# Premaking started later, operand steps and departures regrouped in the down products of an encoder block

## The chip, the cores and the metric

The kernel runs on one core of one Trainium2 chip. The metric is the device time of one execution in microseconds. Engines are named as in the profile: PE (TensorE), DVE (VectorE), ACT (ScalarE), POOL (GpSimd) and SP (SyncE, which only issues DMAs here).

## The reference

One encoder block for 2048 tokens of 1024 channels in float32, cut to what matters here:

```
h  = rmsnorm(x, norm1_g);  p = h @ w_in           # q, k, v, gate, two low-rank decays, u and v of the gMLP
yA = gla_mixer(...)          # chunked gated linear attention, forward and backward over the tokens
yB = gmlp_mixer(...)         # u * (W_s layernorm(v) + b), 128 positions mixed in each of 4 groups
x  = x + concat(yA, yB) @ w_out
h2 = rmsnorm(x, norm2_g)
x  = x + (silu(h2 @ w_gate) * (h2 @ w_up)) @ w_down     # d_ff = 2816
return rmsnorm(x, final_norm_g)
```

## The kernel before

**Tiles and precision.** The channels lie on the 128 partitions, so a block of TB = 512 tokens is KT = 8 tiles of 128x512. The tokens are NB = 4 such blocks. Each float32 product is made of three passes in a faster format, fp32r: every operand is split into a high part (a cast, mostly by ACT) and a low part (the rest, by DVE), and PE multiplies high by high, high by low and low by high.

**Phases.** The first one projects q, k and v and runs the attention forward. The third phase (C; some 310 to 690 us) goes through the blocks 3, 2, 1, 0. For each it makes the z products of the gMLP in a loop of four (the attention's backward steps, `backward`, run beside it: each loads o, ds and q for 128 tokens on SP, scales qb on POOL (L803) and multiplies it on PE as pob (L808)), then the gate and u products, then the eight out products `pout`, n = 0 to 7, with the residual added by DVE as xc (L924). Beside these the next block is normalised (c2h and c2l) and the squares of the new rows are summed (e3sq on ACT, e3a on DVE). The gate and up phase (some 690 to 1630 us) makes the products of a pair of blocks, (3, 2) and then (1, 0), by the Strassen-Winograd scheme: seven products in place of eight, in `seven`, named by slots 0 to 6. The last phase (some 1630 to 2075 us) makes the down products in the same way.

**The down products.** Each pair has three parts, c = 0, 1, 2, of 4, 4 and 3 k-tiles per half. A part is 28 products: one for each of seven slots and each of four column groups q. With 4 k-tiles a product is 12 matmuls of 128x512, with 3 it is 9. In parts 0 and 1 the order is slot 0 four times, slot 4 four times, then slots 3, 1, 2, 6, 5 for each q; in part 2 it is 0 and 4, then 1, 2, 5 for each q, then slot 3 four times and slot 6 four times. A product is named d_ with q and a letter of its bank (d_0e: q = 0). DVE adds the products into acc, one tile for each q, with the steps at L991 and L1152.

**What is loaded and made for them.** The right-hand operands of a part come from DRAM as ac (L1092, SP, eight pieces of 512 KB) and are turned into the seven slots by `moving`, in 22 *operand steps*, each a cast by ACT (L235) and a subtraction by DVE (L236), or one subtraction by DVE (L246). The low and high tiles are named by slot or place: tah and tal, tbh and tbl (slots 0 and 4), s2h and s2l, s5h and s5l, s6h and xf. The tuple `steps` says how many operand steps follow each product of a part; `loads` says after which products a piece of the next part is loaded; `fresh` says after which products the next part's slots 0 and 4 are made.

The left-hand operands of the down products, with the sums of the scheme and both their parts, are *premade* by `make_down` during the third and the gate and up phases: for each set two loads of 512 KB on POOL into mk (L316), seven casts on ACT (L339), four sums (L335) and seven subtractions (L322) on DVE, and the results go to DRAM as dw (L325, POOL). It is a generator: `drain(makes, 1)` runs it to the next `yield`. There are twelve sets (three parts by four q). Later SP loads the results as dn376h, dn376l and so on (L399), in the order of the products.

**The final norm and what leaves.** For one block t of a pair, `square` makes sq (ACT, L1200) of each finished row of acc, and DVE adds most of them into tot. `rstd` multiplies them with ones into fm (L1168, PE), takes the root (ACT, L1170) and the reciprocal (DVE, L1171), and spreads it on a diagonal as tot (L1172); `rows` turns that into rows, fr (L1178, PE), copied back to tot by ACT (L1180). `leave` multiplies acc by it (DVE, L1186) and sends the tile out (L1187). At the change of pairs acc is reused: `residual` (L1160, POOL) loads the next pair's x into it after the old tile has left.

**Order.** In the last phase every engine keeps the order in which the program is written (a chain of dependencies made behind `begin`); `at(n, ...)` puts a call behind product n of a part. PE's banks come from a pool of seven.

## Time and profile before

| | us |
|---|---|
| median of 3 runs | 2097.71 (2095.57 to 2097.91) |
| the profiled execution, its own time | 2099.51 |
| its span, first to last record | 2097.80 |
| PE busy | 2044.1 (97%) |
| DVE busy | 1463.7 (70%) |
| ACT busy | 906.4 (43%) |
| POOL busy | 291.1 (14%) |

The mean granted clock of PE over the span is 0.988. Busy shares are averages over phases with different limits; the list of waits and the table of stretches below show the places.

### The profile page before, as it was taken

What the parts mean: (1) busy time and instruction counts of PE and PEld (TensorE: products, weight loads), DVE (VectorE), ACT (ScalarE), POOL (GpSimd) and SP (SyncE); (2) the same over time, 40 slices, a digit from 0 to 9 for tenths busy, and PEclk for the clock granted to TensorE, in tenths of its full rate; (3) what the DMA queues carried; (4) which work ended last, traced back from release to release, by engine and by line L of the source; (5) the groups of instructions that cost most, each with busy time, mean ns of one, the idle gap of its engine ahead of it and who ended that gap; (6) DMA issues with size and microseconds to landing.
All of it is one profiled execution on the core that took longest, in us unless ns stands there. A gap on an engine that the chain in (4) does not pass through costs nothing. (4 is left out here: it accounts for less than half of the span.)

```text
span 2097.8 us, 25871 instructions
## 1 busy us (share of the span) xinstructions
PE 2044.1 (97%) x9432; PEld 1670.0 (80%) x9432; DVE 1463.7 (70%) x2272; ACT 906.4 (43%) x1560; POOL 291.1 (14%) x487
## 2 busy tenths in 40 slices
PE   8999999999999999999999999999999999899997
PEld 6787877778887888888888888888888888677876
DVE  6977666767767768687766976676667575676576
ACT  6765454464645644343333533333333221431233
POOL 0212223212121100021221001211110100020000
PEclk9999999999999999999999999999999999999998
DMA  8633335555575533254454243433442966687654
GB/s 297 202 113 133 97 136 176 196 190 201 198 268 197 183 121 106 84 177 149 153 176 166 76 146 111 146 138 120 148 147 94 343 220 226 231 312 259 246 173 164
DMA packets 123361, 367.96 MB, mean 175 GB/s; under 512 B 15712, under 2 KB 36064, under 8 KB 121056
## 3 DMA queue, kind: packets, MB, share of 16 engines
q1 hardware_dynamic: 91456, 253.02, 35.1%
q0 software_dynamic: 31632, 112.75, 14.8%
q8 instruction: 74, 1.21, 0.2%
q14 instruction: 55, 0.45, 0.1%
q10 hardware_dynamic: 144, 0.52, 0.1%
HBM read 271.34 MB, written 94.90 MB: 175 GB/s over the span
## 5 line engine op out<-in xcount | busy, mean ns | idle before, releaser
L1079 POOL DMA_DIRECT2D da<-q x88 | 47.6, 541 | 533.6 <-DVE q L1077 511.8
L1055 ACT ACTIVATE cg<-cg 128x512 f32<-128x512 f32 x66 | 41.7, 632 | 118.0 <-DVE cg L1053 117.6
L339 ACT CAST mk<-mk 128x512 fp32r<-128x512 f32 (+1 forms) x84 | 48.9, 583 | 69.0 <-DVE mk L335 50.9
L322 DVE TENSOR_TENSOR mk<-mk 128x512 fp32r<-128x512 f32 (+1 forms) x84 | 56.9, 677 | 15.9 <-DMA dw38l<-mk 2.5
L995 ACT COPY u2d<-d_0a 128x512 f32<-128x512 f32 x6 | 3.5, 584 | 145.7 <-PE d_0a L987 145.7
L235 ACT CAST tah<-ac 128x1024 fp32r<-128x1024 f32 (+1 forms) x24 | 23.4, 977 | 69.1 <-DMA ac<-da 67.5
L617 POOL TENSOR_SCALAR qs<-QK,misc 128x128 f32<-128x128 f32 x30 | 25.6, 856 | 150.8 <-DVE QK L568 76.7
L1077 DVE TENSOR_TENSOR q<-q,cg 128x512 f32<-128x512 f32 x66 | 45.2, 684 | 0.4
L924 DVE TENSOR_TENSOR xc<-pout,xc 128x512 f32<-128x512 f32 x32 | 21.9, 688 | 33.4 <-PE pout L113 33.2
L1200 ACT ACTIVATE sq<-acc 128x512 f32<-128x512 f32 x28 | 17.7, 631 | 61.9 <-DVE acc L1152 61.9
L236 DVE TENSOR_TENSOR tbl<-ac,tbh 128x1024 fp32r<-128x1024 f32 (+1 forms) x24 | 26.3, 1132 | 20.6 <-ACT tbh L235 20.6
L641 DVE SCALAR_TENSOR_TENSOR sf<-sf,misc,dsb 64x128 f32<-64x128 f32 x56 | 19.9, 355 | 23.3 <-ACT dsb L631 22.7
L1187 POOL DMA_DIRECT2D out_dram<-acc x8 | 5.8, 722 | 207.8 <-DVE acc L1186 205.9
L335 DVE TENSOR_TENSOR mk<-mk 128x512 f32<-128x512 f32 (+1 forms) x48 | 34.1, 709 | 0.2
L1152 DVE TENSOR_TENSOR acc<-vvd,acc 128x512 f32<-128x512 f32 x48 | 33.0, 688 | 0.8
L236 DVE TENSOR_TENSOR tal<-ac,tah 128x1024 fp32r<-128x1024 f32 (+1 forms) x24 | 27.0, 1129 | 4.0 <-ACT tah L235 4.0
L818 DVE SCALAR_TENSOR_TENSOR sb<-sb,misc,dsr 128x128 f32<-128x128 f32 x30 | 10.0, 345 | 25.5 <-PE pob L808 24.7
L803 POOL TENSOR_SCALAR qb<-qb,misc 128x128 f32<-128x128 f32 x30 | 19.0, 641 | 62.0 <-DMA qb<-dq 62.0
L624 ACT COPY ot<-po 128x256 f32<-128x256 f32 x32 | 10.3, 373 | 38.7 <-PE po L621 22.0
L246 DVE TENSOR_TENSOR ac<-ac,ac 128x1024 f32<-128x1024 f32 (+1 forms) x24 | 26.7, 1129 | 0.0
L246 DVE TENSOR_TENSOR ac<-ac 128x1024 f32<-128x1024 f32 (+1 forms) x24 | 26.5, 1128 | 0.0
L235 ACT CAST tbh<-ac 128x1024 fp32r<-128x1024 f32 (+1 forms) x24 | 22.5, 981 | 7.0 <-DVE ac L246 6.3
(4609 smaller groups left out, 7358.3 us busy)
## 6 DMA issues: line engine op xcount, KB each, us to landing
da<-q POOLq DMA_DIRECT2D x88, 256.0 KB, 2.3
ac<-da SPq DMA_DIRECT2D x40, 512.0 KB, 6.5
wo<-in_wo_dram SPq DMA_DIRECT2D x32, 512.0 KB, 4.3
xk<-in_xtok_dram SPq DMA_DIRECT2D x16, 512.0 KB, 6.1
wv<-in_wv_dram SPq DMA_DIRECT2D x16, 512.0 KB, 3.5
xc<-in_xT_dram SPq DMA_DIRECT2D x4, 2048.0 KB, 9.6
wg<-in_wg_dram SPq DMA_DIRECT2D x16, 512.0 KB, 3.5
wz<-in_wz_dram SPq DMA_DIRECT2D x16, 512.0 KB, 3.6
```

Source lines behind the costliest of these rows:

```text
L235: nc.scalar.copy(out=hi[:, c, :], in_=src[:, c, :])
L236: nc.vector.tensor_tensor(out=lo[:, c, :], in0=src[:, c, :], in1=hi[:, c, :].bitcast(F32), op=ALU.subtract)
L246: nc.vector.tensor_tensor(out=o[:, c, :], in0=a[:, c, :], in1=b[:, c, :], op=ALU.subtract)
L322: here(nc.vector.tensor_tensor(out=lo.bitcast(F32R), in0=src, in1=hi, op=ALU.subtract))
L335: here(nc.vector.tensor_tensor(out=how[0], in0=how[1], in1=how[2], op=how[3]))
L339: here(nc.scalar.copy(out=hi.bitcast(F32R), in_=src))
L617: nc.gpsimd.tensor_scalar_mul(qs[:, m, :], qd[m][:, c], ech[:, m, 2 * g:2 * g + 1])
L924: nc.vector.tensor_tensor(out=xt[:, n, :], in0=p, in1=xt[:, n, :], op=ALU.add)
L1055: nc.scalar.activation(out=o, in_=a, func=AF.Silu)
L1077: nc.vector.tensor_tensor(out=q, in0=a, in1=cg[:, 2 * m + t, :], op=ALU.mult)
L1079: nc.gpsimd.dma_start(out=d_a[pair[t]][j // KT][:, j % KT, :], in_=q)
L1152: nc.vector.tensor_tensor(out=o, in0=a, in1=o, op=ALU.add)
```

## The change

What it does, in seven pieces:

- *Premaking.* The third phase makes three sets instead of four, and lets four drain steps pass between the loads of a set and its first cast instead of two. Nothing is drained in block 3's z loop, so the first load is issued in its u loop. The gate and up phase makes four sets beside its first pair (as before, but the sets 3 to 6) and five beside its second (50 steps instead of 40).
- *Sums of the norm.* `rstd` first multiplies all terms but the last for four columns, then the last term for four others; ACT copies the first four and DVE adds the second. For pair 0's first block it stands one product later.
- *Pair change.* The first block of pair 0 leaves behind products 25, 26, 27, 27 of its last part (24 to 27 before); the second leaves behind products 4, 5, 13, 15 of the next part (3 to 6 before). Acc is reloaded by one DMA of 512 KB for both halves (`both`) instead of two. The early adds of the first slot in pair 1 stand behind product 13 + q (8 + q before). The operand steps of that part are regrouped.
- *Last parts.* In part 2 the operand steps are 3, 3, 3, 3, 2 instead of seven times 2.
- *Last part of pair 0.* The next part's pieces are loaded behind products 9 to 21 (7 to 20 before) and its slots 0 and 4 made behind 13, 14, 17, 19 (12, 13, 15, 17 before).
- *Last pair.* Two of the four tiles of its first block leave behind products 25 and 26, two behind the last product.
- *Output.* The result is written as (block, partition, tile, token), 4 KB in one piece for each partition of an output DMA, and brought into the reference's form outside the kernel.

```diff
--- before.py
+++ after.py
@@ -50,11 +50,10 @@
     wgu: bass.AP,
     wds: bass.AP,
     wdt: bass.AP,
-    outT: bass.AP,
+    outB: bass.AP,
 ):
     nc = tc.nc
     xv = xT.rearrange("(k p) t -> p k t", p=P)
-    ov = outT.rearrange("(k p) t -> p k t", p=P)
 
     cst = ctx.enter_context(tc.tile_pool(name="cst", bufs=1))
     xp = ctx.enter_context(tc.tile_pool(name="xp", bufs=1))
@@ -305,7 +304,7 @@
 
     d_w = [[drp.tile([P, D], F32, tag=f"dw{j}{x}", name=f"dw{j}{x}") for x in "hl"] for j in range(len(DOWN) // 2)]
 
-    def make_down(c, q, room):
+    def make_down(c, q, room, gap):
 
         hk = PARTS[c]
         w = hk * P
@@ -315,8 +314,8 @@
         for x, r in ((ra, 0), (rb, 1)):
             here(nc.gpsimd.dma_start(out=x, in_=wds[c, 2 * q + r] if c < 2 else wdt[2 * q + r]))
         c1, c2 = slice(0, w), slice(w, 2 * w)
-        yield
-        yield
+        for _ in range(gap):
+            yield
 
         def low(o, src, hi):
             here(nc.vector.tensor_tensor(out=lo.bitcast(F32R), in0=src, in1=hi, op=ALU.subtract))
@@ -344,9 +343,9 @@
 
     MADE = [(c, q) for c in range(len(PARTS)) for q in range(KT // 2)]
 
-    def make_downs(sets, room):
+    def make_downs(sets, room, gap=2):
         for x in sets:
-            yield from make_down(*x, room)
+            yield from make_down(*x, room, gap)
 
     class Stationary:
 
@@ -769,7 +768,7 @@
 
         early = None
 
-        makes = make_downs(MADE[:4], lambda name: pc.tile([P, KT * TB], F32, tag="mk", name=name))
+        makes = make_downs(MADE[:3], lambda name: pc.tile([P, KT * TB], F32, tag="mk", name=name), 4)
         for b in range(NB - 1, -1, -1):
             y = h_tiles(f"y{b}")
             yh, yl = y
@@ -830,7 +829,7 @@
             zps = [big(f"pz{b}_{t}") for t in range(TT)]
             for i in range(4):
                 project_tokens(zps, ws.next(), i, h)
-                drain(makes, int(i < 2))
+                drain(makes, int(b < NB - 1 and i < 2))
                 drain(bw, 1)
                 drain(early, 2)
             drain(bw)
@@ -1102,8 +1101,8 @@
                  for x in ([(0, p) for p in range(3, 9)], [(1, p) for p in range(2, 9)])]
         steps, pieces = {}, []
         for i, x in enumerate(spans):
-            makes = make_downs(MADE[4 + 4 * i:8 + 4 * i], lambda name: xp.tile([P, KT, TB], F32, tag="x2", name=name).rearrange("p k t -> p (k t)"))
-            steps.update({x[len(x) * k // 40]: makes for k in range(40)})
+            makes = make_downs(MADE[3 + 4 * i:(7, 12)[i]], lambda name: xp.tile([P, KT, TB], F32, tag="x2", name=name).rearrange("p k t -> p (k t)"))
+            steps.update({x[len(x) * k // (40 + 10 * i)]: makes for k in range(40 + 10 * i)})
         for n, (i, p, w, o) in enumerate(seq):
             if (i, p, w) not in sets:
                 make = (gate_set, up_set)[w]
@@ -1159,15 +1158,22 @@
         def residual(b, m, t, q):
             nc.gpsimd.dma_start(out=acc[q][:, 2 * t + m, :], in_=d_x[b][:, 2 * q + m, :])
 
+        def both(b, t, q):
+            nc.gpsimd.dma_start(out=acc[q][:, 2 * t:2 * t + 2, :], in_=d_x[b][:, 2 * q:2 * q + 2, :])
+
         def rstd(t, name, terms):
 
             rc = wp.tile([P, D], F32, tag="wraw", name=f"rc{name}", bufs=2)[:, 0:TT]
             m = other(f"fm{name}")
-            for k in range(TT):
-                for n, x in enumerate(terms):
-                    nc.tensor.matmul(out=m[:, k:k + 1], lhsT=x[:, k * P:(k + 1) * P], rhs=ones[:, 0:1],
-                                     start=n == 0, stop=n == len(terms) - 1)
-            nc.scalar.activation(out=rc, in_=m[:, 0:TT], func=AF.Sqrt, bias=eps, scale=1.0 / D)
+
+            for g, xs in enumerate((terms[:-1], terms[-1:])):
+                for k in range(TT):
+                    for n, x in enumerate(xs):
+                        nc.tensor.matmul(out=m[:, g * TT + k:g * TT + k + 1], lhsT=x[:, k * P:(k + 1) * P], rhs=ones[:, 0:1],
+                                         start=n == 0, stop=n == len(xs) - 1)
+            nc.scalar.copy(out=rc, in_=m[:, 0:TT])
+            add(rc, m[:, TT:2 * TT])
+            nc.scalar.activation(out=rc, in_=rc, func=AF.Sqrt, bias=eps, scale=1.0 / D)
             nc.vector.reciprocal(out=rc, in_=rc)
             nc.vector.tensor_tensor(
                 out=total[t].rearrange("p (t j) -> p t j", t=TT), in0=ident.rearrange("p (o j) -> p o j", o=1).broadcast_to([P, TT, P]),
@@ -1184,7 +1190,7 @@
             r = total[t] if r is None else r
             o = acc[q][:, 2 * t:2 * t + 2, :]
             nc.vector.tensor_tensor(out=o, in0=o, in1=r.rearrange("p (o j) -> p o j", o=1).broadcast_to([P, 2, TB]), op=ALU.mult)
-            eng.dma_start(out=ov[:, 2 * q:2 * q + 2, b * TB:(b + 1) * TB], in_=o)
+            eng.dma_start(out=outB[b, :, 2 * q:2 * q + 2, :], in_=o)
 
         Q = range(KT // 2)
         later = {}
@@ -1212,7 +1218,7 @@
                     if b is not None:
                         early(m, t, b)
                     if (c, m, t) == (0, 0, 0):
-                        later.setdefault((i, 0, q + 8), []).append(lambda: early(m, t, a))
+                        later.setdefault((i, 0, q + (8, 13)[i]), []).append(lambda: early(m, t, a))
                         return
                     early(m, t, a)
                     if waiting:
@@ -1231,31 +1237,30 @@
                     at(q, lambda q=q: residual(pair[0], 0, 0, q))
                     for n, (m, t) in zip(((4, 5, 6), (8, 10, 12), (13, 14, 16), (18, 19, 20))[q], ((1, 1), (0, 1), (1, 0))):
                         at(n, lambda q=q, m=m, t=t: residual(pair[t], m, t, q))
-            at(21, lambda i=i, terms=terms: rstd(0, f"{i}_0", terms[0]), C)
-            at(23, lambda i=i: rows(0, f"{i}_0"), C)
+            at((22, 21)[i], lambda i=i, terms=terms: rstd(0, f"{i}_0", terms[0]), C)
+            at((24, 23)[i], lambda i=i: rows(0, f"{i}_0"), C)
             if i == 0:
 
                 old, new = PAIRS[0], PAIRS[1]
                 at(1, lambda terms=terms: rstd(1, "0_1", terms[1]), 0, 1)
                 at(3, lambda: rows(1, "0_1"), 0, 1)
                 for q in Q:
-                    at(24 + q, lambda q=q: leave(old[0], 0, q, nc.gpsimd), C)
-                    at(26 + q if q < 2 else q - 2, lambda q=q: residual(new[0], 0, 0, q), *((C,) if q < 2 else (0, 1)))
-                    at(q, lambda q=q: residual(new[0], 1, 0, q), 0, 1)
-                    at(3 + q, lambda q=q: leave(old[1], 1, q, nc.gpsimd), 0, 1)
-                    at((5, 6, 8, 10)[q], lambda q=q: [residual(new[1], m, 1, q) for m in (1, 0)], 0, 1)
+                    at((25, 26, 27, 27)[q], lambda q=q: leave(old[0], 0, q, nc.gpsimd), C)
+                    at(q, lambda q=q: both(new[0], 0, q), 0, 1)
+                    at((4, 5, 13, 15)[q], lambda q=q: leave(old[1], 1, q, nc.gpsimd), 0, 1)
+                    at((6, 7, 15, 17)[q], lambda q=q: both(new[1], 1, q), 0, 1)
             else:
-                for q in Q:
-                    at(24 + q, lambda q=q: leave(pair[0], 0, q, nc.sync), C)
+                for q in range(2):
+                    at(25 + q, lambda q=q: leave(pair[0], 0, q, nc.sync), C)
 
             for c in range(len(PARTS)):
                 sets = {q: down_set(c, q) for q in Q}
                 j = i * len(PARTS) + c
 
                 change = [j == len(PARTS) + x for x in (0, -1)]
-                steps = (2, 1, 1, 1, 1, 1, 1, 2, 2, 2, 2, 2) if change[0] else (2,) * 7
-                fresh = (12, 13, 15, 17) if change[1] else range(19, 27)
-                loads = (7, 8, 9, 10, 14, 16, 18, 20) if change[1] else (12, 13, 14, 16, 17, 18, 20, 21) if change[0] else range(7, 22, 2)
+                steps = (2, 1, 1, 1, 2, 2, 2, 2, 2, 2, 1) if change[0] else (3, 3, 3, 3, 2) if c == C else (2,) * 7
+                fresh = (13, 14, 17, 19) if change[1] else range(19, 27)
+                loads = (9, 10, 12, 13, 15, 17, 19, 21) if change[1] else (12, 13, 14, 16, 17, 18, 20, 21) if change[0] else range(7, 22, 2)
                 for n, (q, o) in enumerate((q, o) for x, q, o in DOWN if x == c):
                     sets[q][o]()
                     for f in later.pop((i, c, n), ()):
@@ -1269,6 +1274,8 @@
                         pieces.pop(0)()
                     if n in fresh:
                         drain(operands, 1)
+        for q in range(2, 4):
+            leave(pair[0], 0, q, nc.sync)
         rstd(1, "1_1", terms[1])
         r = rows(1, "1_1", False)
         for q in Q:
```

Line numbers behind L57 are smaller by one after the change (L339 becomes L338); `leave` moves from L1186 to L1192.

In ACT's order at the end of block 3's out loop stood this before (e3sq: squares of block 3's new rows, mk: premaking, wz: casts of block 2's first weights):

```order
L87 CAST wz_1h<-wz_1_3900 128x1024
L191 ACTIVATE e3sq_3961<-xc_3307 128x512
L191 ACTIVATE e3sq_3964<-xc_3307 128x512
L339 CAST mk_1_3855<-mk_1_3855 128x512
L191 ACTIVATE e3sq_4024<-xc_3307 128x512
L191 ACTIVATE e3sq_4027<-xc_3307 128x512
L191 ACTIVATE e3sq_4030<-xc_3307 128x512
L87 CAST wz_2h<-wz_2_3967 128x1024
L339 CAST mk_1_3855<-mk_1_3855 128x512
L191 ACTIVATE e3sq_4033<-xc_3307 128x512
```

And this stands there now:

```order
L86 CAST wz_1h<-wz_1_3890 128x1024
L338 CAST mk_0_3395<-mk_0_3395 128x512
L190 ACTIVATE e3sq_3954<-xc_3304 128x512
L190 ACTIVATE e3sq_3957<-xc_3304 128x512
L190 ACTIVATE e3sq_4016<-xc_3304 128x512
L190 ACTIVATE e3sq_4019<-xc_3304 128x512
L190 ACTIVATE e3sq_4022<-xc_3304 128x512
L86 CAST wz_2h<-wz_2_3960 128x1024
L190 ACTIVATE e3sq_4025<-xc_3304 128x512
L338 CAST mk_0_3395<-mk_0_3395 128x512 x2
```

The first cast of a second set stood among the last squares; now the casts there are later ones of the first set, and none stands between the five squares.

On SP, in the last part of pair 0, before (dn: the weights of two products each, numbered as they are loaded; ac: pieces of the next part):

```order
L399 DMA dn374h<-dw33h 128x2x384
L399 DMA dn374l<-dw33l 128x2x384
L1092 DMA ac_0_14421<-da_0_139 128x1024
L399 DMA dn376h<-dw34h 128x2x384
L399 DMA dn376l<-dw34l 128x2x384
L1092 DMA ac_0_14421<-da_0_139 128x1024 x2
L399 DMA dn378h<-dw35h 128x2x384
```

And now:

```order
L398 DMA dn374h<-dw33h 128x2x384
L398 DMA dn374l<-dw33l 128x2x384
L398 DMA dn376h<-dw34h 128x2x384
L398 DMA dn376l<-dw34l 128x2x384
L1091 DMA ac_0_14390<-da_0_139 128x1024
L398 DMA dn378h<-dw35h 128x2x384
```

The weights of dn376 went out behind the first piece of ac; now they go out ahead of it.

On DVE, at the change of pairs, before (tot: the diagonal of the norm, L1186: a leave):

```order
L1172 TENSOR_TENSOR tot_13275<-ident,rc_1_14832 128x512
L246 TENSOR_TENSOR ac_0_14422<-ac_0_14422 128x1024 x2
L1186 TENSOR_TENSOR acc_13270<-acc_13270,tot_13275 128x1024
L236 TENSOR_TENSOR tbl<-ac_0_14421,tbh 128x1024
L1186 TENSOR_TENSOR acc_13271<-acc_13271,tot_13275 128x1024
L236 TENSOR_TENSOR tbl<-ac_0_14421,tbh 128x1024
L1186 TENSOR_TENSOR acc_13272<-acc_13272,tot_13275 128x1024
L246 TENSOR_TENSOR ac_0_14421<-ac_0_14422,ac_0_14421 128x1024
L1186 TENSOR_TENSOR acc_13273<-acc_13273,tot_13275 128x1024
L246 TENSOR_TENSOR ac_0_14421<-ac_0_14422,ac_0_14421 128x1024
L236 TENSOR_TENSOR tbl<-ac_0_14421,tbh 128x1024 x2
L1152 TENSOR_TENSOR acc_13270<-d_0_0c,acc_13270 128x512
```

And now (L1192: a leave):

```order
L1178 TENSOR_TENSOR tot_13275<-ident,rc_1_14831 128x512
L245 TENSOR_TENSOR ac_0_14390<-ac_0_14391 128x1024 x2
L235 TENSOR_TENSOR tbl<-ac_0_14390,tbh 128x1024
L1192 TENSOR_TENSOR acc_13270<-acc_13270,tot_13275 128x1024
L235 TENSOR_TENSOR tbl<-ac_0_14390,tbh 128x1024
L245 TENSOR_TENSOR ac_0_14390<-ac_0_14391,ac_0_14390 128x1024
L1192 TENSOR_TENSOR acc_13271<-acc_13271,tot_13275 128x1024
L245 TENSOR_TENSOR ac_0_14390<-ac_0_14391,ac_0_14390 128x1024
L235 TENSOR_TENSOR tbl<-ac_0_14390,tbh 128x1024 x2
L235 TENSOR_TENSOR s2l<-ac_0_14391,s2h 128x1024 x2
L235 TENSOR_TENSOR xf_6532<-ac_0_14391,s6h 128x1024
L1151 TENSOR_TENSOR acc_13270<-d_0_0c,acc_13270 128x512
```

Two leaves stand where four stood, and the first add into a reloaded acc has come behind three more operand steps.

## Rows read from the trace of the kernel before

**Rows 1.** The page, busy time of each engine, share of the span:

```profile
PE 2044.1 (97%) x9432; PEld 1670.0 (80%) x9432; DVE 1463.7 (70%) x2272; ACT 906.4 (43%) x1560; POOL 291.1 (14%) x487
```

**Rows 2.** Stretches, PE: length, busy (matmuls), granted clock, DMA share, GB/s:

```profile
1900.00:2000.00 100.00, 100.00 (x443) 1.00 0.70 255
323.70:335.20 11.50, 6.29 (x28) 0.70 0.82 271
415.60:422.70 7.10, 3.55 (x10) 0.76 0.44 163
1794.70:1801.70 7.00, 4.87 (x13) 0.76 0.32 97
1803.10:1811.20 8.10, 5.93 (x24) 1.00 1.03 379
1826.60:1836.10 9.50, 7.35 (x27) 0.64 0.47 155
2063.20:2067.10 3.90, 3.90 (x27) 1.00 0.59 201
1879.60:1897.30 17.70, 11.49 (x38) 0.81 0.86 317
2034.60:2040.90 6.30, 4.18 (x11) 0.73 0.37 128
```

**Rows 3.** PE's waits by line: total us, times, longest:

```profile
PE pob L808 <- DMA dsr<-ds: 5.2, 1, 5.2
PE d_0e L985 <- ACT s5h L235: 5.2, 3, 2.5
...
PE pz L111 <- DVE xc L924: 3.6, 1, 3.6
PE fm L1168 <- DVE tot L1152: 2.2, 1, 2.2
...
PE d_1d L985 <- DMA dn376h<-dw34h: 1.1, 1, 1.1
...
PE u_3a L985 <- ACT u2u L995: 0.6, 1, 0.6
```

**Rows 4.** DMA issues of 316 to 324 us: size, median us to landing:

```profile
mk<-in_wds_dram POOLq DMA_DIRECT2D x2, 512.0 KB, 7.6
```

**Rows 5.** Timeline of POOL, 326 to 330 us: start, length, [idle before]:

```profile
328.20 1.85 POOL L803 TENSOR_SCALAR qb<-qb,misc 128x128 f32<-128x128 f32 x3 [9.45 <-DMA qb<-dq]
```

**Rows 6.** Timeline of all engines, 408 to 420 us:

```profile
408.80 1.09 POOL L316 DMA_DIRECT2D mk<-in_wds_dram  x2 [2.03 <-DMA dw6l<-mk]
...
415.38 0.62 ACT L339 CAST mk<-mk 128x512 fp32r<-128x512 f32 x1 [4.39 <-issue]
```

**Rows 7.** Timeline of DVE, 531 to 533 us:

```profile
531.69 1.23 DVE L88 TENSOR_TENSOR wz_0l<-wz,wz_0h 128x1024 fp32r<-128x1024 f32 x1 [2.44 <-ACT wz_0h L87]
```

**Rows 8.** Timeline of DVE, 1790 to 1812 us:

```profile
1796.23 1.83 DVE L236 TENSOR_TENSOR s5l<-ac,s5h 128x1024 fp32r<-128x1024 f32 x2 [1.79 <-ACT s5h L235]
```

**Rows 9.** Timeline of SP, 1795 to 1799 us:

```profile
1798.09 0.33 SPq L1092 DMA_DIRECT2D ac<-da  x1
1798.52 0.52 SPq L399 DMA_DIRECT2D dn376h<-dw34h  x1
```

**Rows 10.** Timeline of DVE, 1863 to 1893 us:

```profile
1864.07 1.23 DVE L1186 TENSOR_TENSOR acc<-acc,tot 128x1024 f32<-128x1024 f32 x1 [5.15 <-ACT tot L1180]
...
1878.16 0.69 DVE L1152 TENSOR_TENSOR acc<-d_0c,acc 128x512 f32<-128x512 f32 x1 [2.57 <-DMA acc<-dx]
...
1891.29 2.35 DVE L236 TENSOR_TENSOR s5l<-ac,s5h 128x1024 fp32r<-128x1024 f32 x2
```

**Rows 11.** Timeline of POOL, 1865 to 1873 us:

```profile
1866.07 0.72 POOL L1187 DMA_DIRECT2D out_dram<-acc  x1 [2.41 <-DVE acc L1186]
...
1871.76 1.10 POOL L1160 DMA_DIRECT2D acc<-dx  x2 [2.88 <-DMA out_dram<-acc]
```

**Rows 12.** Timeline of PE, 2080 to 2087 us:

```profile
2080.65 0.38 PE L1168 MATMUL fm<-ones,sq 128*128 128x1 f32 x2 [1.79 <-ACT sq L1200]
...
2085.89 2.05 PE L1178 MATMUL fr<-tot,ones 128*128 128x512 f32 x2 [1.46 <-DVE tot L1172]
```

5 lines of the change are left out of this document (3 added, 2 removed).

## The prediction

> **What bounds the kernel now.** I read the shares of the engines first: TensorE (PE) is busy 2044.1 of 2097.8 us, VectorE (DVE) 70%, ScalarE (ACT) 43% [rows 1]. So what an edit can give back is time in which PE stands, or runs below its pace. That pace comes from the table of stretches: 443 matmuls in 100.00 us at a granted clock of 1.00, which is 2.4 GHz, take 0.226 us each [rows 2]. Then the list of PE's waits, which says where it stands and for whom: one wait of 5.2 for a DMA (pob), three of 5.2 together for ACT's s5h, and single ones for xc, tot and dn376 [rows 3]. Around each place I took a stretch from the first late matmul to the first that is on pace again, since after each wait the granted clock is also down (0.64 to 0.85 over such a stretch, so part of it at 1.2 GHz). The loss of a place is its length less its matmuls by 0.226. The reader is to see eight such places in rows 2 and a ninth at the tail; the rest of the program is at pace, so moves there are worth nothing unless they break it.
>
> **The change, term by term.** All against the profiled execution, 2099.51 us (span 2097.80), which is 1.8 above the median of the three runs, 2097.71.
>
> 1. *Start of phase C.* pob waits for DMAs whose neighbours are two loads of 512 KB for the premaking, 7.6 us from issue to landing [rows 4]; POOL's qb, which has the same source of delay, comes after 9.45 us of idleness [rows 5]. The stretch of 11.50 us holds 12 matmuls of 512 columns (2.72) and 16 of 128 columns (estimate 1.4), so the loss is 7.3 [rows 2]. The change issues that load later, in block 3's u loop. 1.05 MB at the 271 GB/s of this stretch is 3.9 us of transfer out of the way of a wait of 5.2. About 1.3 stays, with less of the slow clock: gain 5.0 (bounds 0, if the small loads are late by themselves, to 7.3).
>
> 2. *Block 3 to 2.* The load was issued at 408.80, and ACT, which keeps its order, stood 4.39 us at 415.38 in front of the cast that needs it [rows 6]. Behind that cast in ACT's order are the squares on which DVE's sums rest, and behind these DVE's last xc, for which PE waits 3.6 [rows 3]. Loss 7.10 − 10 × 0.226 = 4.8 [rows 2]. With four steps between load and cast, and one whole set in the second half of the out loop, no cast stands there close behind its load. Late next is the last xc itself, behind one more DVE operation of the making. Gain 4.3 (bounds 1.0 to 4.8).
>
> 3. *Blocks 2 to 1 and 1 to 0.* Seven DVE operations of the making now stand before the last out product, where two and three stood: some 5 more, 0.6 each on an engine that never stops between them, so 3.0 us a block. DVE idles 2.44 us there, at 531.69 [rows 7], which covers most. I take −1.5 in all (bounds −6.0, both blocks uncovered, to 0).
>
> 4. *Last part of pair 0.* d_0e waits for s5h; DVE's s5l sits at 1796.23 after 1.79 of idleness, so the order of ACT, not DVE's load, sets it [rows 8]. Loss 7.00 − 13 × 0.226 = 4.1 [rows 2]. Steps of (3,3,3,3,2) end after the fifth product instead of the seventh, two products of 9 matmuls or 4.1 us earlier; the operand steps cost DVE 0.92 each [rows 8], so three beside a product of 2.04 is more than DVE and ACT take at once, and perhaps half of the 4.1 arrives, which is still more than a third of the 5.2 us that d_0e waits in its three places [rows 3]. Gain 3.8 (bounds 1.5 to 4.1).
>
> 5. *dn376.* On SP the load of an activation piece was issued at 1798.09, held back by DVE's reading of that buffer, and the weights of dn376 stood behind it [rows 9]; d_1d waits for them [rows 3]. Loss 8.10 − 24 × 0.226 = 2.7 [rows 2]. Now dn376 is ahead of the first such piece. Gain 2.3 (bounds 0 to 2.7).
>
> 6. *The first sums over channels (fm).* PE waits 2.2 for DVE's tot [rows 3], then multiplies single columns at a low clock: the stretch of 9.50 us holds as many matmuls as one of 3.90 at clock 1.00 [rows 2]. Loss 5.6. One product later (2.04) and with tot's four columns first, the wait goes; an extra ACT copy and a 128x4 DVE add fall beside products. Gain 5.2 (bounds 2.0 to 5.6).
>
> 7. *Pair change.* Loss 17.70 − 38 × 0.226 = 9.1 [rows 2]. DVE is the limit: tot arrives only at 1864.07, four multiplications of 1.23 us follow among the operand steps, DVE waits 2.57 for a reloaded acc, and s5l starts at 1891.29 and takes two steps, until 1893.6 [rows 10]. The change takes out of this stretch two of the four leaves (2.4), four early adds (2.4) and two later adds (1.2): 6.0 of the 27.0 busy us between 1864.07 and 1893.6, so s5l could be done at 1885.1 if DVE never waits. PE without its stalls would start d_0e at 1879.6 + 24 × 0.226 = 1885.0 and want the second half of s5l six matmuls later, 1886.4. What remains is the reload: POOL's out was issued at 1866.07 and had landed at 1871.76, when the two loads behind it went out; the add that uses them ran at 1878.16 [rows 10, 11]. That is 12.1 us; from a first leave that now ends near 1865.3 it gives 1877.4, and DVE needs it (before s5l, after some 12 us of operand steps) at about 1876 to 1878: a wait of 0 to 1.5. So s5l comes 0 to 1.5 late, and I take a gain of 7.0 (bounds 3.0 to 9.1).
> The Trainium skill (page "DMA: Bandwidth & Descriptors", section "Anatomy of one DMA — SWDGE (gpsimd) path") puts a DMA from POOL at about 2.0 us and its bytes over 436 GB/s. For 512 KB that is an estimate of 3.2 us, 6.4 for out and reload, and by it the reload ends long before DVE asks and the term would be 9.1. The 12.1 us of this trace, with the DMA engines at 0.86 a little later [rows 2], disagree with it, and I go by the trace.
>
> 8. *Last part of pair 1.* As 4: 6.30 − 11 × 0.226 = 3.8; gain 3.6 (bounds 1.5 to 3.8) [rows 2].
>
> 9. *Tail.* After the last square, at 2080.65, PE runs all remaining columns of the second sums, until 2085.89 − 1.46 = 2084.4, when DVE can begin tot; fr starts at 2085.89 [rows 12]. With the earlier terms first, 8 single-column instructions remain (0.38 for two, overlapped: about 1.0), done near 2081.7. The extra add must wait for DVE's two deferred leaves (to about 2081.9) and costs some 0.3. fr at 2083.6 instead of 2085.89: gain 2.3 (bounds 1.0 to 4.0, the wider output rows among it).
>
> *At nothing:* the fifth set in pair 1's gate and up products (11 more DVE operations of about 0.69, 7.6 us, over some 270 us in which PE waited once, 0.6, for ACT's u2u [rows 3]); the shifted loads and early operands of pair 0's last part, which keep eight products of 2.04 in hand; POOL's queue, 14% busy [rows 1]. If that cover fails, it is the last rival.
>
> Sum: 5.0 + 4.3 − 1.5 + 3.8 + 2.3 + 5.2 + 7.0 + 3.6 + 2.3 = 32.0. 2099.5 − 32.0 = 2067.5, less 1.8 to the median: **2066 us**. All terms at their best bounds give 41.4, so 2056.
>
> **Rivals.**
> *The waits move on (A).* DVE, freed of one wait, meets the next: at the block changes the added making operations delay the last xc (term 2 gives 1.0, term 3 −3.0), and at the pair change the reload holds DVE (term 7 gives 3.0). For it: DVE limits in both places now, and the reload is 12 us long. Against: DVE idles 2.44 and 5.15 at just these places [rows 7, 10]. 32.0 − 3.3 − 1.5 − 4.0 = 23.2: 2074.5.
> *The start of C stays (B).* dsr and qb are late by the queues' own length, not by the premaking. For it: DMA share 0.82 in that stretch with several small loads among it [rows 2]. Term 1 gives 0: 2070.7.
> *The change doesn't do what it says.* The losses return a product later at every place, since what each waits for moves with the regrouping: about 2098. Against: nine different places would have to agree.
> *Slower.* In pair 1's gate and up phase 50 making steps stand where 40 stood, and DVE's work on the products comes too late for the banks, so that each step costs one wait like that on u2u: 0.6 of idleness [rows 3] and, with the slow clock behind it, about 0.85 (estimate). 50 × 0.85 = 42.5: 2108. From 38 such waits on the gain is gone. Against: at 40 steps there was one.
>
> **How the numbers follow.** Forecast 60% (own range 2058 to 2072), A 20%, B 12%, no effect 4%, slower 4%. The first three are all faster by more than 0.2% (4.2 us, about what a measurement of this kernel can tell from no change): 0.92; same 0.04; slower 0.04. The range runs from just under the best bounds, 2055, past A's 2074.5 with a few us for its own worse ends, to 2080.
>
> **What would show it.** In the profile after: no ACT cast of mk with idle time near 415 and pz gone from PE's waits (2); pob's wait under 2 us (1); no d_0e wait in the two last parts (4, 8); no d_1d wait for dn376 (5); fm behind its product without a pause (6); at the pair change d_0e on time, and DVE's idle time before the first reloaded add under 1.5 us (7); fr some 2 us sooner after the last product (9). A wait of DVE or PE for acc of more than 3 us, a pz or xc wait at a later block change, or repeated u2u waits between 1270 and 1630 us would make it wrong, in the direction of A or of the slower case.

## The result and the profile after

The changed kernel takes 2073.63 us (median of 4 runs, 2069.50 to 2076.67), the one before 2096.88 (4 runs, 2095.57 to 2097.91): a ratio of 0.9888, 95% interval 0.9866 to 0.9910, so 23 us less where 32 were forecast. The profiled execution of the changed kernel is its slowest, 2076.67, with a span of 2074.90.

To see where the time went, the starts of the same matmul in both traces are subtracted, and the difference is read at the bounds of each stage. The forecast column holds the terms of the prediction.

| stage (us in the trace of before) | after less before | forecast |
|---|---|---|
| 0 to 312, reached by no edit | +2.6 | 0 |
| 312 to 405, start of phase C (term 1) | −3.4 | −5.0 |
| 405 to 440, block 3 to 2 (2) | −3.7 | −4.3 |
| 440 to 700, blocks 2 to 1 and 1 to 0 (3) | +2.1 | +1.5 |
| 700 to 1790, gate and up products | +0.9 | 0 |
| 1790 to 1802, last part of pair 0 (4) | −4.3 | −3.8 |
| 1802 to 1812, dn376 (5) | −3.1 | −2.3 |
| 1812 to 1866, fm and fr (6) | +0.3 | −5.2 |
| 1866 to 1899, pair change (7) | −7.6 | −7.0 |
| 1899 to 2042, last part of pair 1 (8) | −4.1 | −3.6 |
| 2042 to the end, tail (9) | −2.5 | −2.3 |
| sum | −22.8 | −32.0 |

The first row is no effect of the change: its stage holds the same instructions in both kernels, and over all profiled executions of this study it lay between 0.4 us shorter and 2.7 us longer than in the trace of before. Without it the change gave 25.4 us. Other stages differ, too, between runs that hold the same instructions there, and this is called their chance range below:

| stage | chance range |
|---|---|
| start of phase C | −2.0 to −3.7 |
| 405 to 700, all block changes | −1.6 to −2.9 |
| gate and up products | −1.1 to +0.9 |
| fm and fr | −1.3 to +1.7 |
| pair change | −7.5 to −9.5 |
| tail | −2.1 to −2.9 |

The profiled execution is at or near the slow end in three of them (block changes, gate and up products, pair change), and the fifth set of the premaking cost nothing that can be told.

The busy time of the engines answers to [rows 1]:

```profile
PE 2035.6 (98%) x9432; PEld 1666.0 (80%) x9432; DVE 1460.6 (70%) x2276; ACT 907.3 (44%) x1564; POOL 282.1 (14%) x479
```

PE's busy time fell by 8.5 us for the same matmuls, which is less time at the lower clock (the mean granted clock went from 0.988 to 0.993). The stretches of the changed kernel that answer to [rows 2] (length, PE busy and matmuls, granted clock, DMA share, GB/s), from the start of phase C to the last part of pair 1:

```profile
326.20:334.40 8.20, 5.67 (x28) 0.79 0.66 199
414.80:418.30 3.50, 2.23 (x10) 1.00 0.22 91
1793.30:1796.00 2.70, 2.70 (x14) 1.00 0.73 218
1797.40:1802.40 5.00, 5.00 (x24) 1.00 0.98 324
1820.90:1833.30 12.40, 9.51 (x40) 0.86 0.32 115
1871.00:1881.10 10.10, 8.84 (x38) 1.00 0.84 291
2018.40:2020.60 2.20, 2.20 (x11) 1.00 0.39 93
```

Both last parts and dn376 are at full pace; the pair change lost 9.1 us and loses 1.5 (10.10 − 38 × 0.226). The fifth row is the one that failed: the stretch of fm still has a low clock (0.86), and fr now stands in it. PE's waits, with those of [rows 3] that stay or are new:

```profile
PE fr L1184 <- DVE tot L1178: 4.5, 2, 2.5
...
PE pz L110 <- DVE xc L923: 3.0, 3, 1.3
PE pob L807 <- POOL qb L802: 2.5, 1, 2.5
...
PE fm L1172 <- DVE tot L1151: 1.3, 1, 1.3
PE d_0e L985 <- DVE s5l L235: 1.3, 2, 0.8
PE u_6a L984 <- ACT u2u L994: 0.9, 1, 0.9
PE u_7a L984 <- ACT u2u L994: 0.8, 2, 0.6
```

The waits for s5h and dn376 are gone, and pz waits three times, once at each block change, where it waited once. New is fr, 2.5 us in pair 0's last part and 2.0 in the tail. What fr waits for stands in ACT's timeline:

```profile
1821.97 1.03 ACT L234 CAST tah<-ac 128x1024 fp32r<-128x1024 f32 x1
1824.89 0.63 ACT L1206 ACTIVATE tot<-acc 128x512 f32<-128x512 f32 x1 [1.89 <-DVE acc L1151]
...
1828.73 0.14 ACT L1174 COPY rc<-fm 128x4 f32<-128x4 f32 x1
1828.89 1.28 ACT L1176 ACT_TABLE_LOAD   x1
1830.19 0.30 ACT L1176 ACTIVATE rc<-rc,eps 128x4 f32<-128x4 f32 x1
```

fm was complete at 1823.2, and ACT copied it 5.5 us later. Ahead of the copy stand three squares with their scalings, and ahead of them an early operand step (the cast at 1821.97) which the change had moved from product 17 to 19. DVE stood for that cast, then subtracted, and only then made the adds that the squares read:

```profile
1823.03 1.23 DVE L235 TENSOR_TENSOR tal<-ac,tah 128x1024 fp32r<-128x1024 f32 x1 [1.79 <-ACT tah L234]
```

The pair change, on POOL and DVE, answers to [rows 10, 11]:

```profile
1859.38 0.54 POOL L1193 DMA_DIRECT2D out_dram<-acc  x1 [5.50 <-DVE acc L1192]
...
1863.58 0.53 POOL L1162 DMA_DIRECT2D acc<-dx  x1 [0.26 <-DMA out_dram<-acc]
```

```profile
1871.44 0.69 DVE L1151 TENSOR_TENSOR acc<-d_0c,acc 128x512 f32<-128x512 f32 x1 [2.34 <-DMA acc<-dx]
...
1878.51 1.22 DVE L235 TENSOR_TENSOR s5l<-ac,s5h 128x1024 fp32r<-128x1024 f32 x1
```

From the issue of out to the add that uses the reload, 12.1 us, as before the change; DVE waits 2.34 for it, and s5l is 1.3 us late in all. The tail answers to [rows 12]:

```profile
2060.07 1.05 PE L1172 MATMUL fm<-ones,sq 128*128 128x1 f32 x8 [0.35 <-ACT sq L1206]
2063.11 2.05 PE L1184 MATMUL fr<-tot,ones 128*128 128x512 f32 x2 [1.98 <-DVE tot L1178]
```

Eight instructions in 1.05 us stand behind the last square, as counted.

### The profile page after: what moved, and what is told of

Read it like the earlier page. It is cut to its first block, busy times and chain, and to the rows that moved or that the text cites. A ratio compares the mean times of both kernels' runs of the same rounds, so it can differ in the third digit from the quotient of the medians.

```text
span 2074.9 us, 25884 instructions
## 1 busy us (share of the span) xinstructions
PE 2035.6 (98%) x9432; PEld 1666.0 (80%) x9432; DVE 1460.6 (70%) x2276; ACT 907.3 (44%) x1564; POOL 282.1 (14%) x479
## 5 line engine op out<-in xcount | busy, mean ns | idle before, releaser
L338 ACT CAST mk<-mk 128x512 fp32r<-128x512 f32 (+1 forms) x84 | 48.9, 582 | 49.3 <-DVE mk L334 33.1
L1206 ACT ACTIVATE sq<-acc 128x512 f32<-128x512 f32 x28 | 17.6, 628 | 44.4 <-DVE acc L1151 44.4
L640 DVE SCALAR_TENSOR_TENSOR sf<-sf,misc,dsb 64x128 f32<-64x128 f32 x56 | 19.9, 355 | 23.5 <-ACT dsb L630 22.8
L235 DVE TENSOR_TENSOR tal<-ac,tah 128x1024 fp32r<-128x1024 f32 (+1 forms) x24 | 27.0, 1130 | 5.8 <-ACT tah L234 5.8
L334 DVE TENSOR_TENSOR mk<-mk 128x512 f32<-128x512 f32 (+1 forms) x48 | 30.8, 641 | 0.2
L245 DVE TENSOR_TENSOR ac<-ac,ac 128x1024 f32<-128x1024 f32 (+1 forms) x24 | 26.7, 1130 | 0.0
L821 ACT ACTIVATE junk<-o 128x128 f32<-128x128 f32 x64 | 19.8, 310 | 13.7 <-issue 5.5
```

The source lines that it names most:

```text
L235: nc.vector.tensor_tensor(out=lo[:, c, :], in0=src[:, c, :], in1=hi[:, c, :].bitcast(F32), op=ALU.subtract)
L245: nc.vector.tensor_tensor(out=o[:, c, :], in0=a[:, c, :], in1=b[:, c, :], op=ALU.subtract)
L334: here(nc.vector.tensor_tensor(out=how[0], in0=how[1], in1=how[2], op=how[3]))
L338: here(nc.scalar.copy(out=hi.bitcast(F32R), in_=src))
```

## The experiments

Single edits of the changed kernel. The times of runs of one kernel lie up to 9 us apart (13 runs of the one before: 2090.59 to 2099.80), so each verdict rests on the stage that its edit reaches, against the trace of before as in the table above.

**Early operand steps back to product 17.**

```diff
-fresh = (13, 14, 17, 19) if change[1]
+fresh = (13, 14, 15, 17) if change[1]
```

> The changed kernel with the last part of pair 0 making the next part's slots 0 and 4 behind products 13, 14, 15, 17 instead of 13, 14, 17, 19. In the changed kernel fr, the product that turns the first norm into rows, waits 2.5 us for tot in that part, and fm before it 1.3. Theory (the queue on ACT): the operand step behind product 19 puts a cast and a subtraction ahead of the squares of d_0c, d_1c and d_2c, and the copy of fm stands behind these squares; with the step gone from there, fr's wait falls from 2.5 to under 0.6, and the kernel gains 2 to 3 us; fm's wait stays near 1.3. Rival (the longer chain of rstd): the added copy, add and hand-overs make fr late; fr's wait stays above 2 us and the time is the same.

Measured: 2070.36 us, ratio to before 0.9876 (0.9853 to 0.9900). The copy of fm stands at the same place in ACT's order, and comes 2.5 us after fm instead of 5.5 (4.5 behind the start of fm; 7.4 in every run with the changed kernel's instructions here); fr runs without a wait:

```profile
1816.92 0.61 ACT L1206 ACTIVATE tot<-acc 128x512 f32<-128x512 f32 x1
...
1820.76 0.14 ACT L1174 COPY rc<-fm 128x4 f32<-128x4 f32 x1
```

```profile
1823.87 1.02 PE L1184 MATMUL fr<-tot,ones 128*128 128x512 f32 x2
```

The stage of fm and fr is 2.9 us shorter than before the change, 3.1 shorter than in the changed kernel; 1.7 of that is a stretch of slow clock behind it (1848 to 1851 us in the changed kernel) that did not occur here and did not in two other runs either, so 1.5 to 3.1 belong to the edit. The theory's mechanism is shown. What it said of fm missed: fm's wait rose from 1.3 to 2.5. The steps that left product 19 stand ahead of fm now; that they delay DVE there is the likely reason, and was not tried.

```profile
PE fm L1172 <- DVE tot L1151: 2.5, 1, 2.5
```

**rstd in one group.**

```diff
-for g, xs in enumerate((terms[:-1], terms[-1:])):
-    for k in range(TT):
-        for n, x in enumerate(xs):
 ...
-nc.scalar.copy(out=rc, in_=m[:, 0:TT])
-add(rc, m[:, TT:2 * TT])
+for k in range(TT):
+    for n, x in enumerate(terms):
 ...
```

> The changed kernel with rstd as it was before (all terms of a column together, no copy and no add), fm and fr still behind products 22 and 24. Rival (the longer chain): fr's wait of 2.5 us in pair 0's last part goes to under 0.6, and only the tail loses. Theory (the queue on ACT): fr's wait falls by the copy and the add alone, 0.4 us, to about 2.1. Both: in the tail all single columns stand behind the last square again, so fr there comes 2 to 3 us later after the last product. Theory: 2 to 2.5 us slower than the changed kernel; rival: within 1 us of it.

Measured: 2071.83 us, ratio 0.9883 (0.9859 to 0.9906). fr's first wait stayed at 2.5, so the copy and the add do not even cost the 0.4 of the theory; the stage stayed (+0.3 and +0.3), and the tail gained 1.8 instead of 2.5. The longer chain is not what made fr late. The grouping is worth 0.3 to 1.1 us in the tail by the chance range, less than the 2 to 3 that both sides expected.

**fr one product later.**

```diff
-at((24, 23)[i], lambda i=i: rows(0, f"{i}_0"), C)
+at((25, 23)[i], lambda i=i: rows(0, f"{i}_0"), C)
-at((25, 26, 27, 27)[q], lambda q=q: leave(old[0], 0, q, nc.gpsimd), C)
+at((26, 26, 27, 27)[q], lambda q=q: leave(old[0], 0, q, nc.gpsimd), C)
```

> The changed kernel with fr behind product 25 of pair 0's last part instead of 24, and the first leave behind 26 instead of 25. Theory: tot is late by a fixed time, so a product of 2.04 us more takes 2 of the 2.5 us of fr's wait away, and the leaves, one product later on DVE, cost the pair change at most 0.5; gain 1.5 to 2. Rival (DVE and ACT are behind altogether, and tot moves with what stands ahead of it): fr's wait stays over 1.5 us, or the pair change gives back as much: s5l late by 2 or more; no gain.

Measured: 2071.43 us, ratio 0.9882 (0.9860 to 0.9905). Of the waits on tot 2.4 are left in two places instead of 4.5. Up to d_1c the stage is 3.3 us shorter than before the change, and loses 3.2 again in two places behind it; at the second the clock is 0.71, with 31 matmuls in the 10 us from 1840, where the changed kernel has 0.83 and 40 (from 1846). The pair change lost nothing (−9.2). The theory had the wait right and not the sum: net −0.1 against +0.3, inside the chance range.

**No premaking in phase C.**

```diff
-makes = make_downs(MADE[:3], lambda ...
+makes = make_downs(MADE[:0], lambda ...
-makes = make_downs(MADE[3 + 4 * i:(7, 12)[i]], lambda ...
-steps.update({x[len(x) * k // (40 + 10 * i)]: makes for k in range(40 + 10 * i)})
+makes = make_downs(MADE[7 * i:(7, 12)[i]], lambda ...
+steps.update({x[len(x) * k // (70 - 20 * i)]: makes for k in range(70 - 20 * i)})
```

> The changed kernel with no premaking in the third phase: seven sets beside the first pair's gate and up products (70 steps instead of 40) and five beside the second as it is. Three questions. (1) pob's wait, 2.5 us in the changed kernel: if the small loads are late by their own queue, it stays at 2 to 2.5; if the premaking's load, now further back, still takes part, it falls under 1. I expect it to stay. (2) PE's waits for xc at the three block changes, 1.3, 0.5 and 1.2 us: if they come from the making operations ahead of the last out product they vanish (gain 3, with the clock behind them); if DVE's own work sets them they stay. I expect them to vanish. (3) The slower case of the prediction: each making step beside gate and up products costs a wait on u2u of 0.6 to 0.9 us; then 30 more steps cost 18 to 27 us. Against it, the steps are hidden and these waits come to under 3 us in all. I expect the second. Together 1 to 4 us faster than the changed kernel.

Measured: 2096.76 us, ratio 0.9999 (0.9989 to 1.0008): the whole gain is gone. (1) pob's wait stays, 2.4. (2) The waits for xc are gone, and 405 to 700 is −5.4 against before, where the changed kernel has −1.6 (chance range to −2.9). (3) The expectation was wrong by far. Between 900 and 1130 us of the trace of before this kernel loses 24.7 us, where the changed one loses 1.2:

```profile
PE u_4a L984 <- ACT u2u L994: 4.9, 1, 4.9
...
PE u_7a L984 <- ACT u2u L994: 3.4, 2, 2.9
PE u_6a L984 <- ACT u2u L994: 3.3, 2, 2.4
PE u_8a L984 <- ACT u2u L994: 3.0, 2, 2.8
PE g_7a L984 <- ACT u2g L994: 2.8, 1, 2.8
```

30 more steps for 23.5 us is 0.78 a step, near the 0.85 of the prediction's slower case. DVE is not full there; a cast of the making waits on ACT, which keeps it in front of the copy that PE needs:

```profile
951.14 0.62 ACT L338 CAST mk<-mk 128x512 fp32r<-128x512 f32 x1 [2.16 <-issue]
...
952.23 0.57 ACT L994 COPY u2u<-u_4a 128x512 f32<-128x512 f32 x1
```

What this cast waits for the profile doesn't name; it began as a sum of the making on DVE (L334, 950.38 and 0.69 long) ended. For the other casts between 930 and 1130 us the list of waits names two things, the sums (9.8 us in seven places in the changed kernel) and the set's own loads (none there):

```profile
ACT mk L338 <- DVE mk L334: 23.3, 10, 5.3
...
ACT mk L338 <- DMA mk<-in_wds_dram: 15.7, 5, 5.6
```

DVE in its turn stood at least 22 us for the writes of dw to leave the one tile that holds the low parts, in the changed kernel 7.5, and POOL, which issues them, is busy 28 us of 100 against 19. So the chain of a set, from load over cast, sum and subtraction to the write, has come too close behind itself; which link to loosen was not tried. So the slower case is real at 70 steps over the 84 products of the first pair that carry them, and absent at 50 over 98 in the second.

**Small loads first.**

```diff
-nc.sync.dma_start(out=lngs, in_=lng)
 ...
+if g < NB * TT - 1:
+    qb = pc.tile([P, 2, P], F32, tag="qb", name=f"qb{g}", bufs=2)
+    nc.sync.dma_start(out=qb, in_=d_q[b][:, :, t * P:(t + 1) * P])
 nc.sync.dma_start(out=o, in_=d_o[g])
 ...
 drain(bw, 1)
+if b == NB - 1 and i == 1:
+    for o, a in ((wss, wsp), (sbias, bsp.partition_broadcast(P)), (lngs, lng), (lnbs, lnb)):
+        nc.sync.dma_start(out=o, in_=a)
```

> The changed kernel with the first loads of the third phase in another order on SP: q of a backward step ahead of its o, and the four constants of the gMLP (0.5 MB) behind the first two backward steps instead of ahead of them. In the changed kernel pob still waits 2.5 us; qb is the ninth DMA that SP issues after the phase's first release, 3.7 us behind it, and lands 5 us later. Theory (the queue on SP): third instead of ninth, qb is issued 2.7 us earlier and lands before PE wants it; pob's wait falls under 0.5, and the stretch gains 2.5 to 3.5 us. Rival (bandwidth: the DMA engines are near full there): the small loads land no earlier, since other bytes go out beside them; the wait stays over 1.5 us.

Measured: 2072.07 us (one run). SP issued qb third, and POOL scaled it at 322.87 instead of 328.18, 4.1 us sooner when the 1.2 us by which this run was ahead at 312 are taken off:

```profile
322.87 1.19 POOL L799 TENSOR_SCALAR qb<-qb,misc 128x128 f32<-128x128 f32 x2 [7.10 <-DMA dsr<-ds]
```

```profile
PE pob L804 <- DMA wss<-in_wsp_dram: 1.9, 1, 1.9
```

Yet pob waits 1.9, and the stage gained 0.3 us, which is inside the chance range. In PE's order pob had stood 15 matmuls behind the first of wz_2; now it stood directly ahead of it. The order of this phase is not that of the program, and it moved pob forward with its loads. (The profile names wss, but pob began at 323.52, as the first of the two scalings ended.) Neither side had that; the queue did set the landing, as the theory said, and it did not set the wait.

**Operand steps of part 2 as before.**

```diff
-(3, 3, 3, 3, 2) if c == C else (2,) * 7
+(2,) * 7
```

> The changed kernel with the operand steps of part 2 as before, seven times two. By the prediction's terms 4 and 8 a wait of about 2.1 us on s5h and s5l comes back at d_0e in both last parts, with the slow clock behind it, 3.8 to 4.1 us at each: 7 to 8.5 us slower than the changed kernel. Rival: other parts of the change (dn376 ahead of the first piece of ac, the pieces two products later) have taken these waits away, and the steps only moved work: under 2 us slower.

Measured: 2080.64 us (one run). The first place is 4.2 us longer than in the changed kernel, the second 4.3, 8.5 together, the upper end of the theory:

```profile
PE d_0e L984 <- ACT s5h L234: 2.7, 2, 1.4
PE d_0e L985 <- DVE s5l L235: 2.3, 3, 0.8
```

dn376 stays on time (−3.1 as in the changed kernel), so terms 4 and 5 are two things. The run shows one thing more. Here PE comes to fm later, fm does not wait for tot, and the stretch up to fr is at full clock:

```profile
1820.30:1829.50 9.20, 6.10 (x35) 1.00 0.55 203
```

```profile
PE fr L1184 <- DVE tot L1178: 5.7, 2, 3.7
```

But fr then waits 3.7 instead of 2.5, and the stage is −0.2, inside its chance range. So fm's wait and the low clock behind it, which term 6 priced, were worth nothing as long as the chain from the squares to fr was late.

**Two loads instead of one.**

```diff
-nc.gpsimd.dma_start(out=acc[q][:, 2 * t:2 * t + 2, :], in_=d_x[b][:, 2 * q:2 * q + 2, :])
+for m in range(2):
+    residual(b, m, t, q)
```

> The changed kernel with each reload of acc at the change of pairs as two DMAs of 256 KB instead of one of 512. In the changed kernel out and reload take 12.0 us from issue to landing (3.9 and 7.8), DVE waits 2.3 us for the first reloaded acc, and s5l makes PE wait 0.8 and 0.5. Theory (size and queues set the time of a DMA): the first half lands 0.5 to 2 us sooner, DVE's wait falls to 0.3 to 1.8, and PE gains 0 to 1.3 us. Rival (a fixed cost for each DMA, so that two cost more than one): the wait grows by 0.5 us or more, and PE loses.

Measured: 2075.64 us (one run). The two halves that the first add needs took 7.8 us from issue to landing (median), as long as the one whole load in the changed kernel, and the second was issued 0.5 behind the first. The first add ran 8.9 us behind the first issue instead of 7.9, DVE waited 3.05 instead of 2.34, and PE's waits for s5l rose from 1.3 to 2.0: the stage is −6.9, 0.6 us outside the chance range. So the gain of the theory did not come. The rival's loss isn't shown: in the run with three edits, which has single loads, DVE waits 3.05 there too, and the stage is −7.0.

**Premaking begun six steps later.**

```diff
 drain(ga, (1, 2, 1, 0)[g])
-drain(makes, 1)
+drain(makes, int(b < NB - 1))
```

> The changed kernel with no premaking step in block 3's u loop, so that the same three sets begin six steps later: a set's loads go out in the second half of a block's out loop, and its casts, sums and subtractions fall in the next block's z and u loops instead of the out loop. In the changed kernel PE waits 1.3, 0.5 and 1.2 us for the last xc of three out loops; without any premaking these waits were gone and the phase was 3.8 us shorter. Theory (DVE is behind in the out loop, and only there): the waits go and the phase is 3 to 4 us shorter. Rival (DVE is as full in the z and u loops, 71%, as it can be, and the squares and gates there become late): a wait of 0.5 us or more at pz, pm or pt in each block; gain under 1 us.

Measured: 2066.21 us (one run). pz is no longer among PE's waits; 405 to 700 is −5.2 us against before, nearly what it is without any premaking there (−5.4), and 2.3 to 3.6 better than the changed kernel by its chance range (−1.6 to −2.9). The gate and up phase (−1.2) is just beyond the fast end of its chance range. No wait appeared in the z and u loops. The theory holds; the run with three edits has the same −5.2.

**The leaves of the pair change early, and then the adds too.**

```diff
-at((4, 5, 13, 15)[q], lambda q=q: leave(old[1], 1, q, nc.gpsimd), 0, 1)
-at((6, 7, 15, 17)[q], lambda q=q: both(new[1], 1, q), 0, 1)
+at(3 + q, lambda q=q: leave(old[1], 1, q, nc.gpsimd), 0, 1)
+at((5, 6, 8, 10)[q], lambda q=q: both(new[1], 1, q), 0, 1)
```

The second kernel has this as well:

```diff
-later.setdefault((i, 0, q + (8, 13)[i]), []).append(lambda: early(m, t, a))
+later.setdefault((i, 0, q + 8), []).append(lambda: early(m, t, a))
```

> The changed kernel with the four leaves of pair 0's second block, and the reloads behind them, where they were before (products 3 to 6, reloads behind 5, 6, 8, 10); the adds of the first slot stay behind product 13 + q. DVE then has two more leaves, 2.4 us, ahead of s5l, and in the changed kernel it waits 2.3 us there for the first reloaded acc. Theory (the reload bounds the pair change): the leaves fill that wait, the first one even goes out sooner, and PE loses under 1 us. Rival (DVE's work bounds it, as term 7 of the prediction counted): s5l comes 2.4 us later and PE loses 2 to 4 us.

> As the run with the leaves early, and the four adds of the first slot also where they were, behind product 8 + q: 4 x 0.6 = 2.4 us more on DVE, of which three adds stand ahead of the last s5l, and each of them needs its own tile reloaded. Theory: here DVE has no idle time left to fill, and waits for each reload in turn: PE's waits at d_0e grow by 2 us or more and the stretch loses 3 to 6 us to the changed kernel, so the later adds, not the later leaves, made most of the gain of the pair change. Rival: the operand steps' new grouping made it, and PE loses under 1 us here as well.

Measured: 2070.75 and 2074.09 us (one run each). The stage is −8.8 with the leaves early and −7.0 with the adds too, against −7.6 in the changed kernel. With the leaves early DVE has no wait left at the first reloaded add:

```profile
1863.89 1.22 DVE L235 TENSOR_TENSOR xf<-ac,s6h 128x1024 fp32r<-128x1024 f32 x1
1865.02 0.68 DVE L1151 TENSOR_TENSOR acc<-d_0c,acc 128x512 f32<-128x512 f32 x1
```

So the reload bounded this place and the leaves only filled its wait. The theory was right for the first kernel. For the second it was wrong: the adds cost 1.8 us against the first, and 0.5 to 2.5 against the chance range, not 3 to 6.

**The grouping of the pair change's steps as before.**

```diff
-(2, 1, 1, 1, 2, 2, 2, 2, 2, 2, 1) if change[0]
+(2, 1, 1, 1, 1, 1, 1, 2, 2, 2, 2, 2) if change[0]
```

> The changed kernel with only the grouping of the operand steps at the change of pairs as before: 2, 1, 1, 1, 1, 1, 1, 2, 2, 2, 2, 2 behind the products of pair 1's first part instead of 2, 1, 1, 1, 2, 2, 2, 2, 2, 2, 1; the later leaves and adds and the joined reloads stay. With the leaves early the changed kernel lost nothing, and with leaves and adds early little. Theory (the grouping made the gain): the first add into a reloaded acc, which waits until some 17.5 us behind fr, then stands ahead of s2l and of all steps behind it instead of ahead of the second xf; s2l comes 2 to 3 us late for d_0d, s5l ends 28 to 31 us behind fr instead of 25.9 (31.2 before the change), and the stretch loses 4 to 7 us to the changed kernel. Rival (each of the pieces covers the same wait, so that any two suffice): under 2 us.

Measured: 2076.02 us (one run). The stage is −2.5 instead of −7.5 to −9.5, so 5 us and more of the gain of the pair change go with the grouping alone. The first add now stands ahead of s2l and holds it and all steps behind it:

```profile
1864.27 0.69 DVE L1151 TENSOR_TENSOR acc<-d_0c,acc 128x512 f32<-128x512 f32 x1 [4.33 <-DMA acc<-dx]
1864.88 1.22 DVE L235 TENSOR_TENSOR s2l<-ac,s2h 128x1024 fp32r<-128x1024 f32 x1
```

```profile
PE d_0e L985 <- DVE s5l L235: 2.1, 1, 2.1
...
PE d_0e L984 <- ACT s5h L234: 1.9, 1, 1.9
```

s5l ends 29.3 us behind fr, inside the theory's 28 to 31.

**Three edits together** (premaking later, early steps behind 12, 14, 15, 17, fr behind 25).

```diff
+drain(makes, int(b < NB - 1))
+fresh = (12, 14, 15, 17) if change[1]
+at((25, 23)[i], lambda i=i: rows(0, f"{i}_0"), C)
+at((26, 26, 27, 27)[q], lambda q=q: leave(old[0], 0, q, nc.gpsimd), C)
```

> The changed kernel with three edits: the premaking of the third phase begun six steps later (as in the run with its steps in the z and u loops), the early operand steps of pair 0's last part behind products 12, 14, 15, 17, which are none of the products whose squares ACT takes, and fr behind product 25 with the first leave behind 26. From the single runs: 3 to 3.5 us in the third phase, 3 for the operand steps, up to 2 for fr where they have not already taken its wait, and fm's wait (1.3 to 2.5) less by what DVE no longer idles for casts (3.0). Together 7 to 9 us faster than the changed kernel; against before a ratio of 0.983 to 0.986. Rival: the edits on fm and fr take the same wait away, and the reload at the pair change, which starts from a later leave, gives 2 us back: 4 to 5 us.

Measured: 2068.13 us (4 runs, 2065.78 to 2069.53), ratio 0.9882 (0.9860 to 0.9904), which can't be told from the changed kernel's 0.9888 (0.9866 to 0.9910); the 0.983 to 0.986 expected was not reached. By stages, the first 312 us left out, it is 8.7 us shorter than the changed kernel's profiled execution, but that one is the slowest of four and this one the fastest of four. 405 to 700 (−5.2) and fm and fr (−3.5) are better than any run of the changed kernel's instructions there, the pair change (−7.0) is worse, and fm still waits 1.9 for tot. By how much it is faster as a whole these runs don't settle.

## Why the prediction was right, and where it was wrong

The sign, the range and the sizes of seven of the nine terms held to within 1 us: 2, 3, 4, 5, 7, 8 and 9. Putting back a single piece confirmed 4 and 8 (8.5 us lost for the 7.4 forecast). Terms 4, 5 and 8 came out 0.2 to 0.4 above their best bounds, so their stretches did not hold the whole loss.

**Term 6 is the step that failed.** "One product later (2.04) and with tot's four columns first, the wait goes; an extra ACT copy and a 128x4 DVE add fall beside products": the wait for tot fell only from 2.2 to 1.3, and the copy did not fall beside products but into ACT's queue, behind three squares which an early operand step, moved by another piece of the same change, had made late. fr then took the wait over. 5.5 of the 6.6 us by which the stages fall short of the sum are this term (3.9 to 6.9 by its chance range). I had put the shift of the early steps among the edits at nothing because their own consumer was eight products away; what counted was who stands behind them on ACT and DVE. The run with that step moved back showed it, and the run with the old steps of part 2 showed the other half: fm without a wait, and nothing gained. The 5.2 came in no run; with the step moved back the stage is −2.9, with fr a product later as well −3.5, and what then holds tot ahead of fm stays open. In the chain behind the copy stands a table load of 1.28 us; the Trainium skill ("ScalarE: Activation LUTs", section "What ACT_TABLE_LOAD costs") gives 1.283 us for it and a drain of 1.38 beside it, of which this trace shows the first alone, the root starting 0.02 us behind the load.

**Term 1 was too large by 1.6.** Taking 1.05 MB out of the way shortened pob's wait from 5.2 to 2.5, not to 1.3. The rest is neither the premaking (the run without any keeps 2.4) nor simply the queue on SP (the run with earlier loads keeps 1.9, at an earlier place in PE's order).

**Term 7 had the size and the wrong cause.** It counted 6.0 us of leaves and adds taken out of DVE's way. With the leaves back nothing is lost and with the adds back at most 2.5, while the grouping of the steps, which the term did not price, is 5 and more. The binding thing was the one the term named last: the reload, 12.1 us from rows of before and 12.1 measured. That match is luck: in the other runs with the same instructions it took 10.2 to 12.2 us from the issue of out to the add, and the stage follows it. In the run with the premaking later, the second fr started at 1845.13 and the first reloaded add 15.8 us behind it, and the stage is −9.5; in the changed kernel it is 17.6 (1853.82 to 1871.44) and −7.6, in the run with two loads 18.3 and −6.9.

```profile
1860.92 0.69 DVE L1151 TENSOR_TENSOR acc<-d_0c,acc 128x512 f32<-128x512 f32 x1 [0.51 <-DMA acc<-dx]
```

So each microsecond of a later reload is one lost here, and the chance range of this stage is that of its reload. The new grouping puts steps ahead of the add that waits for it, and DVE still waited 2.34 where the term had 0 to 1.5. By the Trainium skill ("DMA: Bandwidth & Descriptors", section "Anatomy of one DMA — SWDGE (gpsimd) path") the pair of DMAs would take an estimated 6.4 us and DVE would not wait; it waited 2.34, so the trace was the right side to take.

**Rivals.** The measured 2073.63 lies beside A's 2074.5 by luck: A took 8.8 us from terms 2, 3 and 7 and left term 6 whole. A, that the waits move on, came true in one of its two places: pz waits three times at block changes (term 3, +2.1 for +1.5), and moving the making six steps removes all of it. At the pair change it did not happen. B did not: the premaking's loads were half of that wait. The slower case did not happen at 50 steps but does at 70, at nearly its price; that the cover was close to its end the single u2u wait did not show.

**Two readings.** Rows 2 hold seven places of loss, not eight. The eighth is not priced by any term:

```profile
1855.20:1859.70 4.50, 4.50 (x15) 0.62 1.00 323
```

It is the slow clock behind the second sums that came in some runs and not in others. And the granted clock is not down after each wait: the stretch with dn376's waits is at 1.00 in rows 2.

## What to carry to other kernels

An edit that moves work on an in-order engine is priced by what stands behind it in that order, not by when its own result is wanted; look for the next instruction there that a matmul waits for. A term that comes out right may still have the wrong cause: put back its pieces one by one before building on it. And that a stage stands at 100% PE with one short wait did not tell here how much more could be hidden in it.
